# A gated feed-forward tile is split one iteration later, its low part on GpSimd

## The chip, the cores and the metric

The kernel runs on one core of one Trainium2 chip. The metric is the device time in microseconds (us) of one execution, as the median of several. Engines are named as in the profile: PE is TensorE (matmuls), PEld its weight loads, DVE is VectorE, ACT is ScalarE, POOL (Pool) is GpSimd, SP issues most DMAs.

## The reference

A decoder trunk of two layers over 256 positions of width 1024. Each layer has a mixer (the first one gMLP beside RWKV-7, the second dilated attention) and then a gated feed-forward with a causal convolution of width 3. The change is in the feed-forward alone:

```
def conv_glu_ffn(h, w_up, conv_w, conv_b, w_down):
    z = h @ w_up                       # 1024 -> 2 * 2816
    z1 = shift_prev(z)
    z2 = shift_prev(z1)
    z = conv_w[0] * z2 + conv_w[1] * z1 + conv_w[2] * z + conv_b
    gate, val = jnp.split(z, 2, axis=-1)
    return (jax.nn.silu(gate) * val) @ w_down
```

## The kernel before

Every large matrix product is made from three products of rounded parts. A float32 operand is split into a high part (ACT copies it to the rounded type, line 287 or 246) and a low part (the operand minus the high part, a subtraction by `tt`, line 177, or line 247); `mm3` then adds high times high, high times low and low times high on PE (line 174). `split(hi, lo, src)` at line 286 does this for activations, `load` at lines 244 to 247 for weights. `tt` issues a two-input operation on DVE unless it is given another engine.

Weights come in pieces of up to 128x1024 values. SP loads a piece into `raw` (4 buffers), ACT makes `whi`, DVE makes `wlo` (4 buffers each). `piece()` hands the next one to the matmuls and asks for those up to two ahead. A buffer of `whi` or `wlo` can be written again when PE is done with the piece four before.

`ffn(l, ...)` handles layer l in a loop over FT = 22 tiles. Tile i is 128 gate channels and 128 value channels by 256 positions. Its two pieces take 48 matmuls into one PSUM tile `pg` (3 buffers). Then:

- DVE scales the sums by the norm's row factors into `z` (`z<-pg,rb`, line 177), and POOL has cleared two columns of `z` before (line 974).
- The convolution writes `y`: per half one ACT operation (line 983) and two on DVE (lines 984 and 985).
- ACT applies SiLU to the gate half of `y` (line 986); POOL multiplies it by the value half (`y<-y`, line 177).
- `split` puts the product into `H`: ACT makes the high part (`hh`, line 287), DVE the low part (`hl`, line 177).

`z` and `y` have 3 buffers each, `H` holds all 22 tiles. In layer 0 eight output tiles follow, 22 `mm3` steps each over `H` (`DOWN`: for the first two outputs, tiles 0 to 7, 8 to 14 and 15 to 21 in turn); they read pieces of 8 or 7 tiles, so of 1024 or 896 columns. In layer 1 `finish` does the down-projection with positions as rows, in 128x512 matmuls. In four iterations of layer 1, PE also transposes a part of the residual, and ACT copies it to `Rt`.

Each engine takes its instructions in one fixed order. In the feed-forward that order comes from the scheduler that builds the program; an instruction that waits holds all that stand behind it on its engine.

Of the kernel before, what the change touches and what calls it, by code (L numbers as in the profile page):

```python
# [8 lines left out]
F32 = mybir.dt.float32  # L9
F32R = mybir.dt.float32r  # L10
I32 = mybir.dt.int32
AF = mybir.ActivationFunctionType
OP = mybir.AluOpType
# [7 lines left out]
FT = 22  # L21
# [138 lines left out]
def body(nc, tc, A, out):  # L160
# [3 lines left out]
    V, S, G, PE, SP = nc.vector, nc.scalar, nc.gpsimd, nc.tensor, nc.sync  # L164
# [11 lines left out]
    def tt(o, a, b, op, eng=None):  # L176
        (eng or V).tensor_tensor(o, a, b, op)  # L177
# [14 lines left out]
    def P(k, i=0):  # L192
        return pc[:, _PC[k] + i:_PC[k] + i + 1]
# [39 lines left out]
    def piece():  # L233
        i = used[0]
        used[0] += 1
        while len(made) < min(len(plan), i + 1 + AHEAD):
            made.append(make_piece(*plan[len(made)]))
        w, made[i] = made[i], None
        return w
# [43 lines left out]
                    SP.dma_start(cst[:, :NCE], A["cst"][:, :NCE])  # L283
        return (hi[:, :sz].rearrange("p (k n) -> p k n", k=k), lo[:, :sz].rearrange("p (k n) -> p k n", k=k))

    def split(hi, lo, src):
        S.activation(hi, src, AF.Copy)  # L287
        tt(lo, src, hi.bitcast(F32), OP.subtract)

    def mm3(o, w, wk, ncol, x, xk, start, stop):  # L290
        wh, wl = w[0][:, wk, ncol], w[1][:, wk, ncol]
        xh, xl = x[0][:, xk], x[1][:, xk]
        mm(o, wh, xh, start, False)
        mm(o, wh, xl, False, False)
        mm(o, wl, xh, False, stop)
# [31 lines left out]
    def norm_stats(n, p1=None):  # L327
        if p1 is None:
            p1 = ps.tile([128, 512], F32, name="pst", tag="m", bufs=5)
            p1 = [p1[:, b:b + 1] for b in range(2)]  # L330
            norm_sum(p1, n["acc"], True, True)
        rs = sm.tile([128, 2], F32, name="rs", tag="rs", bufs=2)
        for b in range(2):
            V.tensor_scalar(rs[:, b:b + 1], p1[b], 1.0 / D, 1e-6, op0=OP.mult, op1=OP.add)
        G.tensor_tensor(rs, rs, C("nhalf", 16)[:, 0:2], OP.pow)
        n["rs"] = rs

    def norm_rows(n):
        rs = n["rs"]
        p2 = ps.tile([128, 512], F32, name="prb", tag="m", bufs=5)  # L340
        for b in range(2):
            mm(p2[:, 128 * b:128 * b + 128], rs[:, b:b + 1].to_broadcast([128, 128]), ident)
        rb = sm.tile([128, T], F32, name="rb", tag="rb", bufs=2)
        V.tensor_copy(rb, p2[:, 0:T])
        n["rb"] = rb
        n["rb2"] = rb[:, None, :].to_broadcast([128, 2, T])

    def gps():
        return ps.tile([128, 2, T], F32, name="pg", tag="g", bufs=3)

    def mps():
        return ps.tile([128, 512], F32, name="pm", tag="m", bufs=5)

    def gemm_fm(o, x):

        for g in range(2):
            w = piece()
            for k in range(KT):
                mm3(o[:, g], w, k, slice(0, 128), x, k, k == 0, k == KT - 1)
                yield 327  # L360

    def gemm_first(o, x):

        ws = [piece(), piece()]
        for ks in (range(0, 5), range(5, KT)):
            for g in range(2):
                for k in ks:
                    mm3(o[g], ws[g], k, slice(0, 128), x, k, k == 0, k == KT - 1)
                    yield 327
# [21 lines left out]
    def out_tile(n, gname, d, psrc):  # L391
        tt(R[:, d], R[:, d], psrc, OP.add)
        norm_tile(n, X, gname, d)


    def layer_even(nxt):
# [57 lines left out]
        def projections():  # L454
# [85 lines left out]
            for b in range(2):  # L540
                pp = mps()
                for g in range(4):
                    mm(pp[:, 128 * g:128 * g + 128], vt[:, b, 128 * g:128 * g + 128], wst[:, g])
                bs = slice(128 * b, 128 * b + 128)
                mx = t2("mxd").rearrange("p a (b t) -> p (a b) t", b=2)
                for g in range(4):
                    V.scalar_tensor_tensor(mx[:, g], pp[:, 128 * g:128 * g + 128], P("ln_g", g), bs_[:, g], op0=OP.mult, op1=OP.add)
                tt(u[:, :, bs], mx, u[:, :, bs], OP.mult)
                split(X[0][:, 0:4, bs], X[1][:, 0:4, bs], u[:, :, bs])
                yield 872  # L550
# [290 lines left out]
        def epilogue(h, b, oT):  # L841
            jsl = slice(2 * h, 2 * h + 2)
            bs = slice(128 * b, 128 * b + 128)
            o_ = oT[:, :, bs]
            sqo = sm.tile([128, 2, 128], F32, name="sqo", tag="sqo", bufs=2)
            S.activation(sqo, o_, AF.Square)
            yield ("pe", 0, 0)
            pk = mps()
            for i in range(2):
                mm(pk[:, 2 * i:2 * i + 2], sqo[:, i], C("ind", 2))  # L850
            r2 = sm.tile([128, 4], F32, name="r2", tag="r2", bufs=2)
            rsq(r2, pk[:, 0:4], 1.0 / HD, 64e-5)
            r2e = sm.tile([128, 4, 64], F32, name="r2e", tag="r2e", bufs=1)
            S.copy(r2e, r2[:, :, None].to_broadcast([128, 4, 64]))
            yield ("pe", 430, 0)
            pv = mps()
            for i in range(2):
                mm(pv[:, 128 * i:128 * i + 128], r2e[:, 2 * i:2 * i + 2].rearrange("p a b -> p (a b)"), ident)
            tt(o_, o_, pv[:, 0:256].rearrange("p (j n) -> p j n", j=2), OP.mult)
            tt(o_, o_, gate[:, jsl, bs], OP.mult)  # L860
            tt(o_, o_, v_[:, jsl, bs], OP.add)
            split(YB[h][0][:, :, bs], YB[h][1][:, :, bs], o_)
            yield ("pe", 440, 0)
            if b == 1:
                when[f"yb{h}"], WHEN[f"yb{h}"] = clock[0], cnt[0]
# [91 lines left out]
    def ffn(l, n, nxt, gname):  # L957
        pool = tc.tile_pool(name=f"ff{l}", bufs=1)
        fp = pool.__enter__()
        H = [fp.tile([128, FT, T], F32R, name=f"h{x}{l}") for x in "hl"]  # L960
        if l == 1:
            Rt = fp.tile([128, 2, D], F32, name="Rt")
            last["pool"] = fp
        for i in range(FT):
            o = [gps()[:, 0], gps()[:, 0]] if i == 0 else gps()
            for y_, _ in enumerate(gemm_first(o, X) if i == 0 else gemm_fm(o, X)):
                if i == 0 and y_ == 9:
                    norm_stats(n)
                if i == 0 and y_ == 14:
                    norm_rows(n)  # L970
            z = fp.tile([128, 2, T + 2], F32, name="z", tag="z", bufs=3)
            if i == 0:
                fp.tile([128, 248], F32, name="pad_z")
            G.memset(z[:, :, 0:2], 0.0)  # L974
            if i == 0:
                for g in range(2):
                    tt(z[:, g, 2:T + 2], o[g], n["rb"], OP.mult)
            else:
                tt(z[:, :, 2:T + 2], o, n["rb2"], OP.mult)
            y = fp.tile([128, 2, T], F32, name="y", tag="y", bufs=3)  # L980
            for g in range(2):
                ch = i + FT * g
                S.activation(y[:, g], z[:, g, 2:T + 2], AF.Identity, scale=P(f"cw{l}2", ch), bias=P(f"cb{l}", ch))  # L983
                V.scalar_tensor_tensor(y[:, g], z[:, g, 1:T + 1], P(f"cw{l}1", ch), y[:, g], op0=OP.mult, op1=OP.add)  # L984
                V.scalar_tensor_tensor(y[:, g], z[:, g, 0:T], P(f"cw{l}0", ch), y[:, g], op0=OP.mult, op1=OP.add)  # L985
            S.activation(y[:, 0], y[:, 0], AF.Silu)  # L986
            tt(y[:, 0], y[:, 0], y[:, 1], OP.mult, G)
            split(H[0][:, i], H[1][:, i], y[:, 0])
            if l == 1 and i in (2, 3, 4, 5):
                b, e = i % 2, (i - 2) // 2  # L990
                pt = mps()
                for d in range(4):
                    PE.transpose(pt[:, 128 * d:128 * d + 128], R[:, 4 * e + d, 128 * b:128 * b + 128], ident)
                S.copy(Rt[:, b, 512 * e:512 * e + 512], pt)
        if l == 1:
            finish(H, fp, Rt)
            pool.__exit__(None, None, None)
            return
        os = {}
        for d, k0, kn in DOWN:  # L1000
            if k0 == 0:
                os[d] = gps()[:, 0]
            w = piece()
            for k in range(kn):
                mm3(os[d], w, k, slice(0, 128), H, k0 + k, k0 + k == 0, k0 + k == FT - 1)
            if k0 + kn == FT:
                out_tile(nxt, gname, d, os.pop(d))
        pool.__exit__(None, None, None)
# [189 lines left out]
    n3 = norm_new()  # L1198
    layer_odd(n2, n3)
    ffn(1, n3, None, None)  # L1200
    ctx.close()

# [12 lines left out]
```

## Time and profile before

| | us |
|---|---|
| median of 3 runs (674.57 to 676.83) | 675.12 |
| the profiled execution | 676.43 |
| its span, first to last instruction | 674.7 |
| PE busy (5766 matmuls) | 644.9 (96%) |
| DVE busy (946 instructions) | 509.2 (75%) |
| ACT busy (710) | 394.5 (58%) |
| POOL busy (154) | 108.8 (16%) |

The up-projection loop of layer 0 lies at about 183 to 312 us of the span, its down-projection reaches to about 372 us, the loop of layer 1 lies at about 486 to 613 us. Busy shares are means over all stages; the chain that ended last and the waits inside one stage tell more. Ends of matmuls are modelled and overlap, so the distance from start to start is the pace of PE.

### The profile page before, as it was taken

To read this page: it belongs to the slowest core of one execution; us is meant where nothing else is said; L and a number is where in the kernel's file an instruction comes from. 1 tells how busy PE (TensorE), PEld (TensorE's weight loads), DVE (VectorE), ACT (ScalarE), POOL (GpSimd) and SP (SyncE) were. 2 spreads that over 40 slices of the span, in tenths; PEclk is the share of its full clock that TensorE was granted. 3 is DMA by queue.
4 is the path that set the end of the run, shared out by engine and by line. 5 is a ranking of instruction groups with operands and counts; after the bars stand their busy time and mean duration, and the time that the engine had idled before them with its cause. 6 is when DMAs were issued, how large, how long until landed. Compare 5 with 4: busy or idle time off the path is not lost.

```text
span 674.7 us, 14452 instructions
## 1 busy us (share of the span) xinstructions
PE 644.9 (96%) x5766; PEld 615.4 (91%) x5766; DVE 509.2 (75%) x946; ACT 394.5 (58%) x710; POOL 108.8 (16%) x154
## 2 busy tenths in 40 slices
PE   7998989799899999999999999999999999999996
PEld 6888767679899999999999999998999999998896
DVE  6899966747888888888766379886888888888653
ACT  6776432324666666666544468766576666666531
POOL 4100000110422222221112000001222222221000
PEclk9998999879999999999999999999999999999998
DMA  7747264203455555555767553332755555555741
GB/s 250 249 145 235 71 177 103 64 2 126 139 174 177 171 185 175 172 176 167 248 195 222 164 181 126 125 126 95 236 186 177 184 168 177 187 164 195 235 126 63
DMA packets 44916, 110.33 MB, mean 164 GB/s; under 512 B 16433, under 2 KB 18097, under 8 KB 44849
## 3 DMA queue, kind: packets, MB, share of 16 engines
q1 hardware_dynamic: 31104, 105.03, 48.3%
q10 hardware_dynamic: 13584, 3.86, 2.3%
q8 instruction: 45, 0.74, 0.5%
q0 software_dynamic: 160, 0.52, 0.3%
q14 instruction: 23, 0.18, 0.1%
HBM read 106.50 MB, written 2.90 MB: 162 GB/s over the span
## 4 chain that ended last, share of the span: by engine, by line
PE 65%; DVE 20%; POOL 5%; ACT 4%; issue 3%; DMA 3%; SPq 0%; POOLq 0%; ACTq 0%; DVEq 0%
PE pg L174 50%; PE pm L174 14%; DVE wlo L247 6%; POOL y L177 3%; DVE WR L177 2%; DVE y L984 2%; DVE z L177 2%; ACT y L986 1%; DVE y L985 1%; ACT hh L287 1%; DMA scrA<-BK 1%; DVE ftmp L177 1%; PE pm L1135 1%; DVE xl L304 1%; DMA R<-xT 1%
## 5 line engine op out<-in xcount | busy, mean ns | idle before, releaser
L174 PE MATMUL pg<-xh,whi 128*128 128x256 f32 x1008 | 290.0, 288 | 0.6 <-ACT whi L246 0.6
L174 PE MATMUL pg<-xh,wlo 128*128 128x256 f32 x1008 | 284.4, 282 | 2.3 <-DVE wlo L247 2.3
L174 PE MATMUL pg<-xl,whi 128*128 128x256 f32 x1008 | 284.3, 282 | 0.1
L247 DVE TENSOR_TENSOR wlo<-raw,whi 128x1024 fp32r<-128x1024 f32 (+2 forms) x199 | 233.9, 1181 | 46.8 <-ACT whi L246 46.3
L246 ACT ACTIVATE whi<-raw 128x1024 fp32r<-128x1024 f32 (+2 forms) x199 | 200.7, 1017 | 72.2 <-PE pg L174 48.8
L174 PEld LDWEIGHTS pg<-xh,whi 128*128 128x128 f32 x1008 | 192.5, 191 | 6.3 <-issue 3.9
L174 PEld LDWEIGHTS pg<-xh,wlo 128*128 128x128 f32 x1008 | 190.9, 189 | 3.1 <-DVE wlo L247 3.1
L174 PEld LDWEIGHTS pg<-xl,whi 128*128 128x128 f32 x1008 | 192.7, 191 | 0.8 <-DVE xl L300 0.3
L177 POOL TENSOR_TENSOR y<-y 128x256 f32<-128x256 f32 x44 | 63.6, 1445 | 29.2 <-ACT y L986 28.7
L287 ACT ACTIVATE hh<-y 128x256 fp32r<-128x256 f32 x44 | 18.4, 417 | 71.2 <-POOL y L177 71.2
L983 ACT ACTIVATE y<-z,pc 128x256 f32<-128x256 f32 x88 | 48.2, 595 | 9.0 <-DVE z L177 3.9
L177 DVE TENSOR_TENSOR hl<-y,hh 128x256 fp32r<-128x256 f32 x44 | 18.7, 425 | 45.3 <-ACT hh L287 45.3
L174 PE MATMUL pg<-hh,wlo 128*128 128x256 f32 x176 | 49.1, 279 | 0.6 <-DVE wlo L247 0.6
L174 PE MATMUL pg<-hh,whi 128*128 128x256 f32 x176 | 48.7, 277 | 0.0
L174 PE MATMUL pg<-hl,whi 128*128 128x256 f32 x176 | 48.7, 277 | 0.0
L177 POOL TENSOR_TENSOR sqacc<-sqacc,sq 128x256 f32<-128x256 f32 x21 | 18.6, 886 | 162.0 <-ACT sq L312 161.5
L984 DVE SCALAR_TENSOR_TENSOR y<-z,pc,y 128x256 f32<-128x256 f32 x88 | 38.6, 479 | 0.8 <-ACT y L983 0.8
L985 DVE SCALAR_TENSOR_TENSOR y<-z,pc,y 128x256 f32<-128x256 f32 x88 | 38.7, 478 | 0.1
L174 PEld LDWEIGHTS pg<-hh,wlo 128*128 128x128 f32 x176 | 33.0, 188 | 1.3 <-DVE wlo L247 1.2
L174 PEld LDWEIGHTS pg<-hh,whi 128*128 128x128 f32 x176 | 33.1, 188 | 0.0
L174 PEld LDWEIGHTS pg<-hl,whi 128*128 128x128 f32 x176 | 33.1, 188 | 0.0
L974 POOL MEMSET z<- 128x4 f32 x44 | 4.2, 103 | 170.2 <-ACT y L986 151.9
(247 smaller groups left out, 1041.4 us busy)
## 6 DMA issues: line engine op xcount, KB each, us to landing
raw<-w_up SPq DMA_DIRECT2D x88, 512.0 KB, 3.5
raw<-w_dn SPq DMA_DIRECT2D x30, 512.0 KB, 4.1
raw<-w_qkv SPq DMA_DIRECT2D x24, 512.0 KB, 4.0
raw<-w_in SPq DMA_DIRECT2D x20, 512.0 KB, 4.9
raw<-w_dn SPq DMA_DIRECT2D x16, 448.0 KB, 3.9
raw<-ev_wo SPq DMA_DIRECT2D x8, 512.0 KB, 3.8
raw<-od_wo SPq DMA_DIRECT2D x8, 512.0 KB, 3.9
R<-xT SPq DMA_DIRECT2D x4, 256.0 KB, 3.9
```

What stands on the lines that cost most here:

```text
L174: PE.matmul(o, l, r, start=start, stop=stop, skip_group_check=shared)
L177: (eng or V).tensor_tensor(o, a, b, op)
L246: S.activation(hi[:, c], raw[:, c], AF.Copy)
L247: last["lo"] = V.tensor_tensor(lo[:, c], raw[:, c], hi[:, c].bitcast(F32), OP.subtract).ins
L287: S.activation(hi, src, AF.Copy)
L304: V.scalar_tensor_tensor(x[1][:, k], R[:, k], P(gname, k), x[0][:, k].bitcast(F32), op0=OP.mult, op1=OP.subtract)
L974: G.memset(z[:, :, 0:2], 0.0)
L983: S.activation(y[:, g], z[:, g, 2:T + 2], AF.Identity, scale=P(f"cw{l}2", ch), bias=P(f"cb{l}", ch))
L984: V.scalar_tensor_tensor(y[:, g], z[:, g, 1:T + 1], P(f"cw{l}1", ch), y[:, g], op0=OP.mult, op1=OP.add)
L985: V.scalar_tensor_tensor(y[:, g], z[:, g, 0:T], P(f"cw{l}0", ch), y[:, g], op0=OP.mult, op1=OP.add)
L986: S.activation(y[:, 0], y[:, 0], AF.Silu)
L1135: PE.transpose(pt[:, 128 * i:128 * i + 128], sc[:, 128 * i:128 * i + 128], ident)
```

## The change

Inside the loop, tile i's `split` no longer follows its own gating. The tile is kept in a dictionary `ys`, and one iteration later its high part is queued on ACT behind the SiLU of the next tile (`issue_after` fixes that order on ACT), and its low part goes to POOL instead of DVE. The last tile is still split at once, on ACT and DVE.

```diff
-    def split(hi, lo, src):
+    def split(hi, lo, src, eng=None):
         S.activation(hi, src, AF.Copy)
-        tt(lo, src, hi.bitcast(F32), OP.subtract)
+        tt(lo, src, hi.bitcast(F32), OP.subtract, eng)
...
+        ys = {}
         for i in range(FT):
...
-            S.activation(y[:, 0], y[:, 0], AF.Silu)
+            silu = S.activation(y[:, 0], y[:, 0], AF.Silu).ins
             tt(y[:, 0], y[:, 0], y[:, 1], OP.mult, G)
-            split(H[0][:, i], H[1][:, i], y[:, 0])
+
+            ys[i] = y
+            if i > 0:
+                with tc.issue_after(silu):
+                    split(H[0][:, i - 1], H[1][:, i - 1], ys.pop(i - 1)[:, 0], G)
+            if i == FT - 1:
+                split(H[0][:, i], H[1][:, i], ys.pop(i)[:, 0])
```

Seven lines are new ahead of the loop's convolution and SiLU, so line 984 of before is 985 after, 985 is 986, 986 is 987 and 974 is 975. The order of PE's and of SP's instructions is the same in both programs. On DVE, in the middle of the loop of layer 0 (`hl_2260` and `hh_2259` are the two parts of `H`), before:

```order
301 L247 TENSOR_TENSOR wlo<-raw,whi 128x1024
302 L177 TENSOR_TENSOR hl_2260<-y,hh_2259 128x256
303 L177 TENSOR_TENSOR z<-pg,rb 128x2x256
304 L247 TENSOR_TENSOR wlo<-raw,whi 128x1024
305 L984 SCALAR_TENSOR_TENSOR y<-z,pc,y 128x256 x2
306 L985 SCALAR_TENSOR_TENSOR y<-z,pc,y 128x256 x2
```

and now:

```order
303 L247 TENSOR_TENSOR wlo<-raw,whi 128x1024
304 L177 TENSOR_TENSOR z<-pg,rb 128x2x256
305 L247 TENSOR_TENSOR wlo<-raw,whi 128x1024
306 L985 SCALAR_TENSOR_TENSOR y<-z,pc,y 128x256 x2
307 L986 SCALAR_TENSOR_TENSOR y<-z,pc,y 128x256 x2
```

Nothing of the split stands in DVE's queue any more, but for the last tile of each layer. On POOL, at the same place, before:

```order
60 L177 TENSOR_TENSOR y<-y 128x256
61 L974 MEMSET z 128x2x2
62 L177 TENSOR_TENSOR y<-y 128x256
63 L974 MEMSET z 128x2x2
64 L177 TENSOR_TENSOR y<-y 128x256
```

and now:

```order
61 L975 MEMSET z 128x2x2
62 L177 TENSOR_TENSOR y<-y 128x256
63 L177 TENSOR_TENSOR hl_2260<-y,hh_2259 128x256
64 L975 MEMSET z 128x2x2
65 L177 TENSOR_TENSOR y<-y 128x256
66 L177 TENSOR_TENSOR hl_2260<-y,hh_2259 128x256
```

Each `y<-y` of one tile is followed by the low part of the tile before it. On ACT, at the end of the loop of layer 0 (the last two tiles and the first pieces of the down-projection), before:

```order
282 L983 ACTIVATE y<-z,pc 128x256 x2
283 L246 ACTIVATE whi<-raw 128x896
284 L986 ACTIVATE y<-y 128x256
285 L287 ACTIVATE hh_2259<-y 128x256
286 L246 ACTIVATE whi<-raw 128x896
```

and now:

```order
281 L984 ACTIVATE y<-z,pc 128x256 x2
282 L246 ACTIVATE whi<-raw 128x896
283 L987 ACTIVATE y<-y 128x256
284 L287 ACTIVATE hh_2259<-y 128x256 x2
285 L246 ACTIVATE whi<-raw 128x896
```

The `hh` behind a SiLU is now that of the tile before it, and at the end two of them stand in a row, of the last tile but one and of the last.

## Rows read from the trace of the kernel before

**Rows 1.** Chain that ended last, one period of layer 0's loop: start, duration (us), what

```profile
260.61 1.48 POOL y L177
262.11 0.43 ACT hh L287
262.90 0.68 DVE z L177
263.59 1.15 DVE wlo L247
265.96 0.43 ACT y L986
```

**Rows 2.** Windows: length, each engine's busy time (instructions), PE clock, DMA share, GB/s

```profile
190.44:310.57 120.13, 120.08 (x1020) 119.87 (x1019) 98.20 (x161) 77.30 (x122) 32.07 (x39) 1.00 0.54 174
318.00:372.00 54.00, 54.00 (x476) 54.00 (x477) 36.44 (x42) 28.08 (x40) 9.63 (x12) 1.00 0.71 217
```

**Rows 3.** Timeline of DVE, layer 0's loop: start, duration, instruction, idle before and releaser

```profile
190.44 0.69 DVE L177 TENSOR_TENSOR z<-pg,rb 128x512 f32<-128x512 f32 x1 [0.34 <-PE pg L174]
310.57 0.68 DVE L177 TENSOR_TENSOR z<-pg,rb 128x512 f32<-128x512 f32 x1
```

**Rows 4.** Timeline of PE's weight loads, layer 0, behind the loop's last up-projection

```profile
306.17 0.19 PEld L174 LDWEIGHTS pg<-hl,whi 128*128 128x128 f32 x1
306.62 0.19 PEld L174 LDWEIGHTS pg<-hh,wlo 128*128 128x128 f32 x1 [0.26 <-DVE wlo L247]
...
311.62 0.19 PEld L174 LDWEIGHTS pg<-hl,whi 128*128 128x128 f32 x1
312.31 0.19 PEld L174 LDWEIGHTS pg<-hh,wlo 128*128 128x128 f32 x1 [0.50 <-DVE wlo L247]
...
314.59 0.19 PEld L174 LDWEIGHTS pg<-hl,whi 128*128 128x128 f32 x1
314.89 0.19 PEld L174 LDWEIGHTS pg<-hh,wlo 128*128 128x128 f32 x1
...
317.24 0.19 PEld L174 LDWEIGHTS pg<-hl,whi 128*128 128x128 f32 x1
317.90 0.19 PEld L174 LDWEIGHTS pg<-hh,wlo 128*128 128x128 f32 x1 [0.47 <-DVE wlo L247]
```

**Rows 5.** The same timeline behind layer 1's loop, and that loop's window

```profile
620.56 0.19 PEld L174 LDWEIGHTS pm<-wlo,hh 128*128 128x128 f32 x1 [0.18 <-DVE wlo L247]
...
492.39:612.70 120.31, 120.31 (x998) 119.14 (x997) 98.34 (x163) 78.84 (x127) 32.06 (x39) 1.00 0.55 176
```

**Rows 6.** Timelines of POOL and DVE, three places where POOL's two-input operation ran

```profile
190.42 0.75 POOL L177 TENSOR_TENSOR y<-y 128x256 f32<-128x256 f32 x1 [1.23 <-ACT y L986]
...
272.21 1.22 DVE L247 TENSOR_TENSOR wlo<-raw,whi 128x1024 fp32r<-128x1024 f32 x1
272.56 1.47 POOL L177 TENSOR_TENSOR y<-y 128x256 f32<-128x256 f32 x1
...
343.85 1.23 DVE L247 TENSOR_TENSOR wlo<-raw,whi 128x1024 fp32r<-128x1024 f32 x1 [0.61 <-ACT whi L246]
344.66 1.01 POOL L177 TENSOR_TENSOR sqacc<-sqacc,sq 128x256 f32<-128x256 f32 x1 [6.47 <-ACT sq L312]
344.99 0.96 DVE L304 SCALAR_TENSOR_TENSOR xl<-R,pc,xh 128x256 fp32r<-128x256 f32 x1
```

**Rows 7.** Timelines of ACT and DVE around tile 1 of layer 0

```profile
193.20 1.06 ACT L246 ACTIVATE whi<-raw 128x1024 fp32r<-128x1024 f32 x1 [0.47 <-ACT y L983]
194.25 0.42 ACT L986 ACTIVATE y<-y 128x256 f32<-128x256 f32 x1
194.53 1.22 DVE L247 TENSOR_TENSOR wlo<-raw,whi 128x1024 fp32r<-128x1024 f32 x1
```

**Rows 8.** Windows where each layer's up-projection starts, columns as in rows 2

```profile
180.00:186.00 6.00, 5.36 (x32) 5.16 (x32) 4.26 (x7) 2.12 (x2) 1.62 (x1) 0.72 0.61 191
480.00:486.00 6.00, 5.33 (x46) 5.12 (x45) 3.69 (x7) 2.43 (x4) 2.03 (x6) 1.00 0.86 291
```

## The prediction

> **What bounds the kernel now.** I read the chain that ended last first. In layer 0's loop it doesn't run through PE but around a circle of three engines: POOL multiplies `y` (260.61), ACT makes `hh` (262.11), DVE, which had to wait for `hh` before it could take `hl`, scales the next `z` (262.90), makes a `wlo` (263.59), convolves, ACT takes the SiLU (265.96), and POOL follows [rows 1]. Each tile's split so holds DVE back from the next tile.
>
> The second view says what that circle costs. In the 120.13 us from the scaling of tile 1 to that of tile 21, PE is busy for 120.08 us and starts 1020 matmuls [rows 2]. That is 0.1178 us for each; the 20 tiles between need 20 x 48 = 960, and the other 60 already belong to the down-projection. So PE needs 48 x 0.1178 = 5.65 us for a tile and the circle takes 120.13 / 20 = 6.01 us. At the start, DVE waited 0.34 us for PE, so it was not behind; at tile 21 it is behind by 60 x 0.1178 = 7.07 us [rows 3]. PE doesn't stand still for that in the loop, since it runs ahead on weights that were split early. The loop is thus bound by two things at once: PE sets the time, the circle eats up PE's stock of split weights.
>
> The bill comes at the end of the loop, where PE waits for the `wlo` that stand in DVE's late queue [rows 4]. There are four places. From the weight load before to the one that came late it took 0.45, 0.69, 0.30 and 0.66 us, 2.10 in all, where the pace would be 4 x 0.118 = 0.47. **PE lost 1.63 us there.** Behind that, PE is busy for the whole 54.00 us of the down-projection [rows 2]. In layer 1 the loop's window is busy for 120.31 of 120.31 us, and there is a single wait for a `wlo` behind it, of 0.18 us [rows 5].
>
> **The change part by part.**
>
> *Removed from DVE:* 42 of the 44 `hl` (one per tile but for each layer's last), with the wait for `hh` in front of each. The circle is cut: `z` of the next tile stands behind a `wlo` alone. DVE's busy time per tile was 98.20 / 20 = 4.91 us [rows 2]; it was the wait that made 6.01 of it. Without them DVE needs less than PE's 5.65, so it follows PE and never falls behind. PE's order and SP's are unchanged, no matmul goes away and no DMA. The gain is then what PE waited at the ends of the loops and no more: 1.63 + 0.18 = **1.81 us**. The other 20 x 0.36 us that the circle loses are hidden behind a busy PE and are worth nothing.
>
> *Moved to ACT's place behind the next SiLU:* the same 44 `hh`, 0.43 us each [rows 1]. ACT no longer waits for POOL there, so the move costs nothing; ACT's own work is 77.30 / 20 = 3.87 us per tile [rows 2].
>
> *Added to POOL:* 42 two-input operations of 128x256. The trace has no `hl` on POOL. The nearest rows are POOL's `y` and `sqacc`, same size, and they differ: 0.75, 1.47 and 1.01 us [rows 6]. Set beside DVE's rows they tell why. The 0.75 ran beside a DVE operation that reads PSUM (`z`, 190.44 [rows 3]), and neither was longer than usual. The 1.47 began at 272.56, while a `wlo` with both inputs in SBUF ran, whose work ends at 272.21 + 1.15 = 273.36; 0.67 us after that `y` was done. The third began at 344.66 inside a `wlo` that ended at about 345.0, and was done 0.67 later; the DVE operation with two SBUF inputs that was issued at 344.99 then took 0.96 us and ended 0.28 behind POOL. So two-input operations of the two engines pass one after the other, and POOL's own work is 0.67 to 0.75 us. Bounds for one `hl`: 0.67 from below, 1.47 from above if the row's whole length were work. I take 0.7, since it is the value that explains all three.
>
> Does POOL then hold DVE up? Tile 1 was on time, so it shows the steady state that I expect [rows 7]. Counted from the start of its `z` at 190.44: a `whi` starts at 2.76 (its buffer comes free only as PE finishes one more piece, 24 x 0.118 = 2.83), SiLU runs from 3.81 to 4.23, a `wlo` from 4.09 to 5.24. POOL's `y` is issued at about 4.35, passes behind the `wlo` and ends near 5.95. The moved `hh` is long there (4.23 + 0.43 = 4.66), so `hl` runs from 5.95 to 6.65. In that time DVE does the next `z`, at 5.65, from PSUM, beside POOL. The next two-input operation on DVE is a `wlo` whose `whi` has to wait for PE to finish a piece at 5.65 and takes 1.06, so it starts at 6.7. `hl` fits into the hole with about 0.05 us to spare, and if it doesn't, DVE has 5.65 - 5.24 = 0.41 us of its own idle time per tile. Nothing is lost until POOL's delay exceeds that by more than 0.36, the drift that is there now.
>
> *Held longer:* `y` of tile i is read by POOL one tile later, so its buffer (3 of them) comes free at about 6.65 after the next tile's `z`; the writer is tile i + 3 on ACT, two tiles after that. No wait. At the end, the last `hh` stands on ACT behind POOL's last `y`, at about 5.95 after the last `z`, with a `whi` for the down-projection's sixth piece behind it. PE by its order first does five pieces, 8 + 8 + 7 + 7 + 7 steps of three matmuls or 111 x 0.118 = 13.1 us; that `whi` and its `wlo` are done by about 8.5. `H` of the last two tiles is wanted in the sixth and seventh step of the fifth piece, 12.4 us or more behind that `z`, and is there at about 7. Both are covered by 4 us or more; without the cover each would be a stall of that size.
>
> **The sum.** The profiled execution took 676.43 us, 1.3 above the median of 675.12. 676.43 - 1.81 = 674.62 for it, and for the median 675.12 - 1.81 = **673.3 us**, 0.27% less. A difference under 0.3% (2.0 us) is about what a measurement of this kernel can't tell from none. So the change does what it says, the gain is real by the trace, and it lies just inside that bound.
>
> **The rivals.**
>
> *The drift stays in part* (0.16). If `hl` lands on the `wlo` behind `z`, DVE loses up to 0.7 us per tile, 0.41 of it idle anyway, so 0.29 of drift remain where 0.36 were. 20 x 0.29 = 5.8 us instead of 7.07, so the waits shrink by 1.3 at most, and could by less. Against it speaks the hole of [rows 7]; for it, that the hole is only as long as `hl`. Time: 673.9 to 674.9.
>
> *POOL becomes the bound: slower* (0.05). If 1.47 us were POOL's own work and it kept DVE's two-input operations out for all of it, a tile would need 2 x 1.47 = 2.94 us of POOL beside DVE's 4.91 - 0.42 (`hl`) - 0.68 (`z`) = 3.81, so 6.75 us, a drift of 1.1 per tile. Over 20 tiles that is 22 us; from 7.07 the stall now grows one for one, so 15 us more in each layer: about 705 us. It turns slower where the two POOL operations take together over 6.01 - 3.81 = 2.2 us. The 0.75 of [rows 6] speaks against it. The Trainium skill's page "Perfetto Trace Analysis" (Optimizing Scalar/DVE Operations) warns that DVE and GpSimd share an SBUF read port, so that moving work between the two might not help; the rows show the shared passage, but also that the moved operation falls into a time where DVE reads PSUM.
>
> *PE's clock falls once more* (0.11). Ahead of layer 0's first tile, PE stood and was then granted 0.72 of its speed on average in 180 to 186 us; at the same place of layer 1 it stood less and kept 1.00 [rows 8]. Everything there now comes 1.6 us earlier. If layer 1 fell to the level of 1.2 GHz as layer 0 did, 0.28 x 6 = 1.7 us would go and eat the gain: 675.0. The wait in front of it doesn't change, so I don't expect it.
>
> *More comes back than was read* (0.08). Waits that depend on where weights stand in the queues at the start of the attention could shorten too: 671 to 672.5. The full 54.00 us between leaves little for that.
>
> **How the numbers follow.** The forecast (672.7 to 674.0) has 0.60, the rivals 0.16, 0.05, 0.11 and 0.08. The bound of 0.3% is at 673.1, a little under the forecast, and runs differ by more than that distance: I give 0.4 of the forecast's 0.60 and all of the last rival to "faster", 0.32. "Slower" is POOL as the bound and a small part of the clock's case, 0.07. The rest is 0.61. The range of 8 in 10 takes in the drift and the clock above and the first half of the last rival below: 671.8 to 675.6.
>
> **What would show it.** Right: `z` one tile after the other at 5.65 us instead of 6.01, with waits for PE in front of it; no weight load behind layer 0's loop that waits for `wlo`; POOL with `y` and `hl` back to back, `hl` of about 0.7 us. The moved step is wrong if `wlo` behind `z` starts when `hl` ends, or `z` still comes later than PE. The sum is wrong if the four late weight loads stay though DVE is on time (then it was the transfer or ACT that they waited for), or if the down-projection of layer 0, busy throughout before, shows new gaps.

## The result, and the profile after

The changed kernel takes **670.82 us** (median; 20 runs, 664.22 to 677.61). The kernel before took 676.65 us (20 runs, 674.57 to 678.24). The ratio is **0.9896, 95% interval 0.9875 to 0.9918**: 1.0% faster, where 0.3% was forecast, and below the range. Five of the changed kernel's 20 runs (674.83 to 677.61) are so far above its fastest that the ratio leaves them out (with them the medians stand at 0.9914, 0.9% faster); the one profile of this kernel taken at such a time (678.34 us) shows the slower of the two paces that are told of below.

The profiled execution took 672.47 us, 3.96 less than that of before (676.43). The windows of the changed kernel cover the 19 tiles from the scaling of tile 2 of layer 0 to that of tile 21, its down-projection behind that, and a part of layer 1's loop (columns as in [rows 2]):

```profile
197.44:300.81 103.37, 103.37 (x914) 103.37 (x913) 87.95 (x134) 70.60 (x115) 42.97 (x57) 1.00 0.60 192
300.81:360.33 59.52, 59.52 (x527) 59.52 (x526) 38.57 (x44) 30.66 (x43) 8.78 (x9) 1.00 0.65 196
523.00:600.00 77.00, 77.00 (x656) 77.00 (x655) 64.19 (x97) 51.14 (x82) 29.18 (x39) 1.00 0.58 186
```

PE is busy throughout, as in [rows 2], at the same granted clock of 1.00. But a tile of layer 0 takes 103.37 / 19 = **5.44 us**, not the 5.65 that I forecast: a matmul takes 103.37 / 914 = 0.1131 us where before it took 0.1178. In layer 1 it takes 77.00 / 656 = 0.1174, the old pace. So the trace of one and the same kernel holds two paces for the same matmul at the same clock.

The timeline of DVE in the changed kernel shows who waits for whom (start, duration, instruction, idle before and releaser), over one period of layer 0 and one of layer 1:

```profile
251.84 0.69 DVE L177 TENSOR_TENSOR z<-pg,rb 128x512 f32<-128x512 f32 x1 [0.46 <-PE pg L174]
252.88 1.23 DVE L247 TENSOR_TENSOR wlo<-raw,whi 128x1024 fp32r<-128x1024 f32 x1 [0.34 <-ACT whi L246]
254.02 0.88 DVE L985 SCALAR_TENSOR_TENSOR y<-z,pc,y 128x256 f32<-128x256 f32 x2
255.60 1.22 DVE L247 TENSOR_TENSOR wlo<-raw,whi 128x1024 fp32r<-128x1024 f32 x1
257.28 0.69 DVE L177 TENSOR_TENSOR z<-pg,rb 128x512 f32<-128x512 f32 x1 [0.46 <-PE pg L174]
...
596.34 0.69 DVE L177 TENSOR_TENSOR z<-pg,rb 128x512 f32<-128x512 f32 x1 [0.63 <-PE pg L174]
602.00 0.69 DVE L177 TENSOR_TENSOR z<-pg,rb 128x512 f32<-128x512 f32 x1 [0.63 <-PE pg L174]
```

Each `z` now waits for PE, still in the last tiles; in [rows 3] the later `z` had long found its sums done. No `hl` stands on DVE here. The groups of POOL's instructions in layer 0's loop (count, busy us, mean ns, then idle time before) and two rows of POOL's timeline:

```profile
L177 POOL TENSOR_TENSOR y<-y 128x256 f32<-128x256 f32 x22 | 31.2, 1417 | 11.7 <-ACT y L987 10.8
L177 POOL TENSOR_TENSOR hl<-y,hh 128x256 fp32r<-128x256 f32 x20 | 14.9, 744 | 0.0
...
250.52 1.46 POOL L177 TENSOR_TENSOR y<-y 128x256 f32<-128x256 f32 x1
251.94 0.74 POOL L177 TENSOR_TENSOR hl<-y,hh 128x256 fp32r<-128x256 f32 x1
```

`hl` takes 744 ns, as the shortest of [rows 6], stands back to back with `y`, and begins within 0.1 us of DVE's `z` at 251.84, which keeps its 0.69 us.

Where the 3.96 us went: from the first `z` to the last matmul of layer 0's down-projection it is 187.79 to 360.33 = 172.5 us, against 185.89 to 364.95 = 179.1 before, so 6.5 less. In this execution the part ahead of that was 1.9 us longer, with the same code. The attention between took 123.3 us in both. From layer 1's first `z` to the end it took 187.0 us, against 186.4 before: layer 1 gained nothing here, it lost 0.6. (The counts of a window include one or two matmuls that only touch its edges.)

### The profile page after: what moved, and what is told of

Read it like the earlier page. It is cut to its first block, busy times and chain, and to the rows that moved or that the text cites. A ratio compares the mean times of both kernels' runs of the same rounds, so it can differ in the third digit from the quotient of the medians.

```text
span 670.6 us, 14493 instructions
## 1 busy us (share of the span) xinstructions
PE 642.1 (96%) x5766; PEld 613.1 (91%) x5766; DVE 500.4 (75%) x904; ACT 390.6 (58%) x710; POOL 136.4 (20%) x196
## 4 chain that ended last, share of the span: by engine, by line
PE 79%; DVE 12%; DMA 3%; issue 2%; ACT 1%; POOL 1%; ACTq 1%; SPq 0%; POOLq 0%; DVEq 0%
PE pg L174 63%; PE pm L174 14%; DVE wlo L247 3%; DVE WR L177 2%; DMA scrA<-BK 1%; DVE ftmp L177 1%; PE pm L1142 1%; DVE xl L304 1%; DMA R<-xT 1%; DMA at<-scrA 1%; DMA raw<-w_up 1%; ACTq L706 0%; PE prb L174 0%; DVE BK L662 0%; POOL r L321 0%
## 5 line engine op out<-in xcount | busy, mean ns | idle before, releaser
L177 POOL TENSOR_TENSOR y<-y 128x256 f32<-128x256 f32 x44 | 61.7, 1401 | 27.7 <-ACT y L987 26.8
L177 DVE TENSOR_TENSOR z<-pg,rb 128x512 f32<-128x512 f32 (+1 forms) x46 | 30.5, 667 | 21.3 <-PE pg L174 21.3
L177 POOL TENSOR_TENSOR hl<-y,hh 128x256 fp32r<-128x256 f32 x42 | 31.2, 742 | 0.0
```

## The experiments

The theory that the texts on record call FLOOR: PE does the 128x256 matmul, with its weight load, at one of two paces, 113.3 or 117.8 ns, and keeps one for a whole stretch. The circle of three engines ([rows 1], 5.97 us per tile once it turns steadily) lay above both, 48 x 0.1133 = 5.44 and 48 x 0.1178 = 5.65 us, and so was a floor under the loop that hid the pace. The deferral removes the floor, and then the time shows the pace. The rivals: that POOL's relief of DVE makes the gain, and that the faster pace is luck of an execution, which the kernel before could have drawn as well.

**The deferral without POOL** (in the changed kernel):

```
-                    split(H[0][:, i - 1], H[1][:, i - 1], ys.pop(i - 1)[:, 0], G)
+                    split(H[0][:, i - 1], H[1][:, i - 1], ys.pop(i - 1)[:, 0])
```

> Only the deferral: the split of a gated tile comes one iteration later, behind the next SiLU, but its low part stays on DVE. Theory FLOOR: the three-engine circle (6.01 us per tile) was a floor under the loop, and PE has two paces, 113.3 and 117.8 ns per matmul, of which it keeps one for a whole loop; cutting the circle is all that counts. DVE then needs 4.9 us per tile, less than 48 x 113.3 ns = 5.44, so this is as fast as the changed kernel: 664 to 677 us from run to run, median 669 to 673. Rival POOL: the faster pace of PE comes from taking the low part off DVE; then PE stays at 117.8 ns and the time is 673 to 676.

Measured: 670.1 us (8 runs, 667.91 to 677.29), ratio 0.9926 (0.9888 to 0.9964), beside the 0.9914 that the changed kernel has over all its runs. The window over 19 tiles of this kernel and three rows of its DVE:

```profile
195.43:298.45 103.02, 103.02 (x911) 103.02 (x910) 94.77 (x154) 70.50 (x115) 35.14 (x36) 1.00 0.61 192
...
253.25 1.22 DVE L247 TENSOR_TENSOR wlo<-raw,whi 128x1024 fp32r<-128x1024 f32 x1
254.38 0.42 DVE L177 TENSOR_TENSOR hl<-y,hh 128x256 fp32r<-128x256 f32 x1
254.93 0.69 DVE L177 TENSOR_TENSOR z<-pg,rb 128x512 f32<-128x512 f32 x1
```

`hl` is back on DVE, in front of `z`, but waits for nothing, since its `hh` is a tile old. 103.02 / 19 = 5.42 us per tile: the deferral alone does it.

**POOL without the deferral** (in the kernel before):

```
-            split(H[0][:, i], H[1][:, i], y[:, 0])
+            split(H[0][:, i], H[1][:, i], y[:, 0], G)
```

> Only the other engine: the low part on POOL, but the split at once, as before. Theory FLOOR: the circle now closes through ACT, whose high part still waits for POOL's product and has a weight piece behind it: SiLU 0.43, POOL 1.95 with its wait, high part 0.43, whi 1.05, wlo 1.15, convolution 1.2, so about 6.2 us per tile. That is a floor like that of before: 674 to 680 us with a small spread. Rival POOL: PE at 113.3 ns, 664 to 673.

Measured: 677.19 us (12 runs, 675.53 to 678.99), ratio 1.0009 (0.9995 to 1.0023). DVE is relieved (494.4 us busy in its profile, where it was 509.2) and nothing is gained. The timelines of this kernel's ACT and DVE, one turn:

```profile
268.70 0.42 ACT L287 ACTIVATE hh<-y 128x256 fp32r<-128x256 f32 x1 [1.71 <-POOL y L177]
269.02 1.04 ACT L246 ACTIVATE whi<-raw 128x1024 fp32r<-128x1024 f32 x1
...
270.10 1.22 DVE L247 TENSOR_TENSOR wlo<-raw,whi 128x1024 fp32r<-128x1024 f32 x1 [1.43 <-ACT whi L246]
...
272.54 0.42 ACT L986 ACTIVATE y<-y 128x256 f32<-128x256 f32 x1 [0.54 <-DVE y L985]
274.68 0.42 ACT L287 ACTIVATE hh<-y 128x256 fp32r<-128x256 f32 x1 [1.72 <-POOL y L177]
```

The circle goes on through ACT: `hh` waits for POOL, the `whi` behind it and then DVE's `wlo` come late, then the convolution, SiLU and POOL. From `hh` to `hh` it is 274.68 - 268.70 = 5.98 us (6.2 was expected). The wait that has to go is ACT's for POOL, and of the two halves of the change only the deferral removes it.

**Both kernels once more**, unchanged, to see whether an execution draws its pace.

> The kernel before, unchanged, once more, for a second profile. Theory FLOOR: 674.5 to 678.5 us whatever PE's pace; if this profile has a loop at 113.3 ns, its tiles still come every 5.97 us and the waits for weights behind that loop add up to more, up to 6 us instead of 1.6. Rival POOL: PE is at 117.8 ns in both loops.

> The changed kernel, unchanged, for a second profile. Theory FLOOR: each loop is either at 113.3 or at 117.8 ns by chance and its tiles come every 5.44 or 5.65 us; the time is about 664 with both fast, 670 to 672 with one, 676 with none. Rival POOL: layer 0 at 113.3 and layer 1 at 117.8 as in the first profile, 670 to 672.

Measured: 678.11 and 678.34 us (one run each). The kernel before: two windows of its layer 0 loop, then a weight load and two `z` between them from the timelines:

```profile
198.79:253.00 54.21, 54.21 (x481) 54.21 (x480) 44.49 (x74) 34.95 (x55) 14.21 (x18) 1.00 0.56 177
260.00:312.00 52.00, 50.34 (x418) 48.54 (x418) 42.29 (x71) 32.88 (x53) 13.98 (x16) 1.00 0.53 169
...
254.47 0.19 PEld L174 LDWEIGHTS pg<-xh,wlo 128*128 128x128 f32 x1 [0.42 <-DVE wlo L247]
...
252.59 0.68 DVE L177 TENSOR_TENSOR z<-pg,rb 128x512 f32<-128x512 f32 x1
258.56 0.68 DVE L177 TENSOR_TENSOR z<-pg,rb 128x512 f32<-128x512 f32 x1
```

This time PE began at 54.21 / 481 = 0.1127 us and ran ahead; at 254.47 its stock of split weights was used up, and from there it stood still once per tile. `z` comes every 5.97 us all the same. The floor, seen directly: the fast pace was there, and bought nothing. The changed kernel, in the same two stretches as above:

```profile
196.78:304.19 107.41, 107.41 (x914) 107.41 (x913) 89.02 (x133) 70.54 (x115) 41.90 (x57) 1.00 0.59 184
304.00:366.00 62.00, 62.00 (x529) 62.00 (x528) 38.68 (x44) 30.69 (x43) 8.80 (x9) 1.00 0.64 188
```

107.41 / 914 = 0.1175 us in the loop, 62.00 / 529 = 0.1172 behind it: no wait for a `wlo` anywhere, and yet no faster than before. With `z` on time, and PE at 5.65 us per tile, it is the kernel of my forecast, and shows the second half of my mistake, below.

**The floor put back** (in the changed kernel): three more operations on DVE per tile, behind the convolution, whose result nobody reads, so that DVE has more work than PE.

```
+        scr = fp.tile([128, T], F32, name="scr")
...
+            with tc.issue_after(conv):
+                for _ in range(3):
+                    V.scalar_tensor_tensor(scr, z[:, 1, 0:T], P(f"cw{l}0", ch), y[:, 1], op0=OP.mult, op1=OP.add)
```

> The changed kernel with three idle convolution steps more per tile on DVE (0.40 us each, written to a scratch tile that nothing reads), which neither ACT nor POOL waits for. DVE then needs 4.5 + 1.2 = 5.7 us per tile, up to 6.5 where it passes behind POOL's operations. Theory FLOOR: the floor is back without the circle; tiles come every 5.75 to 6.5 us whatever PE's pace, PE waits for weights at the end of the loop or once per tile, and the time is 675 to 695 us, tile time and waits fitting each other. If only PE's pace by itself mattered, the time would stay at 664 to 678 with a median near 671.

Measured: 694.48 us (4 runs, 692.55 to 695.61), ratio 1.0262 (1.0237 to 1.0287). A window of this kernel's loop and two `z`:

```profile
240.00:300.00 60.00, 58.90 (x474) 55.27 (x473) 60.00 (x100) 36.05 (x60) 25.26 (x30) 1.00 0.53 172
...
255.78 0.68 DVE L177 TENSOR_TENSOR z<-pg,rb 128x512 f32<-128x512 f32 x1
261.90 0.68 DVE L177 TENSOR_TENSOR z<-pg,rb 128x512 f32<-128x512 f32 x1
```

DVE is busy for 60.00 of 60.00 us and the tiles come every 6.12 us (6.62 in layer 1), though nearly all of PE's stretches in this loop ran at 113.3 ns. A floor above PE sets the time, also where it is built of work, not of waits.

**The pace asked for.** In the six profiles up to here, the matmuls behind the attention's 64-column matmuls ran at 113.3 ns. (That those behind every broadcast ran at 117.8, as the expectation below has it, is not so: layer 0's first loop stands behind one, with a stretch at half clock at its start, and ran at 113.3 in three of the six.) So I put two small, unneeded matmuls of 64 columns ahead of each loop's stretch and behind the four transposes in layer 1, in the changed kernel and in the one before:

```
+    def drain():
+        pd = mps()
+        for q in (slice(0, 64), slice(64, 128)):
+            mm(pd[q, 0:64], ident[:, 0:64], ident[:, 0:64])
```

> The changed kernel with two idle matmuls of 64x64 (nothing reads their result) behind the norm's broadcast at the start of each loop and behind the four transposes in layer 1. In six profiles PE ran at 113.3 ns per matmul behind every stretch of 64-column matmuls in the attention and at 117.8 behind every broadcast or transpose. Theory FLOOR with the pace set by what PE did last: both loops and layer 0's down-projection run at 113.3, tiles every 5.44 us in both layers, 663 to 667 us with a small spread. If the pace is chance: as the changed kernel, 664 to 678, plus about 0.5.

> The kernel before with the same idle matmuls. Theory FLOOR: PE may start at 113.3 ns but uses up its stock of split weights in some 13 tiles and then waits once per tile; tiles stay at 5.97 us and the time stays at 674 to 679, as without them. If the circle were no floor, both loops would gain from the pace and the time would be 664 to 670.

Measured: the changed kernel so drained takes 668.53 us (6 runs, 666.04 to 675.84), ratio 0.989 (0.9848 to 0.9932). That misses the 663 to 667 of "what PE did last", and two of the six runs lie above 675: both fit the expectation's other case, a pace drawn by chance. The kernel before so drained takes 677.37 us (12 runs, 673.91 to 678.6), ratio 1.001 (0.9993 to 1.0027). It ran at 113.3 ns from 186.3 us to 258 in layer 0 and from 518 to 591 in layer 1, then waited, and stayed at 5.97 and 5.98 us per tile: a faster PE is worth nothing under the floor. The waits in layer 0 of the drained kernel before (us in all, times, longest):

```profile
PEld pg L174 <- DVE wlo L247: 4.3, 11, 0.5
```

The profiled execution of the drained changed kernel took 675.71 us. Its windows, layer 0's loop and down-projection and then layer 1's loop:

```profile
196.00:304.00 108.00, 108.00 (x919) 108.00 (x918) 89.82 (x135) 71.30 (x117) 42.09 (x57) 1.00 0.58 185
305.20:367.20 62.00, 62.00 (x529) 62.00 (x528) 38.65 (x44) 30.69 (x43) 8.83 (x9) 1.00 0.63 188
522.00:606.00 84.00, 84.00 (x743) 84.00 (x742) 71.19 (x109) 57.52 (x93) 33.45 (x45) 1.00 0.60 193
```

Layer 1 runs at 84.00 / 743 = 0.1131, layer 0 at 0.1175. Its drain had stood in front of a stretch at half clock (181.4 to 188.2 us), and behind that the pace came out slow. (In the drained kernel before, the same drain with a shorter such stretch behind it, 182.4 to 185.8 us, was followed by the fast pace.) So I put one more drain behind layer 0's first tile, and one ahead of the attention's values:

```
+            if l == 0 and i == 1:
+                drain()
```

> The changed kernel with the idle 64x64 matmuls of the run before, and two places more: behind tile 1 of layer 0, where PE is back at full clock, and behind the norm's broadcast at the start of the attention layer. Theory FLOOR with the pace set by what PE did last: the loops of both layers at 113.3 ns and 5.44 us per tile in every execution, 664 to 668 us, none above 670. If the pace is chance, some executions stay above 672, as four of six of the run before were not.

Measured: 668.8 us (6 runs, 667.02 to 671.63), ratio 0.9882 (0.9853 to 0.9912). No run is left near 675, but one is above the 670 expected, and the median is 0.8 us above the expected 664 to 668. In the profile both loops run fast, layer 0's at 100.00 / 884 = 0.1131 us:

```profile
200.00:300.00 100.00, 100.00 (x884) 100.00 (x884) 84.96 (x130) 67.93 (x112) 42.11 (x55) 1.00 0.60 193
515.00:598.00 83.00, 83.00 (x734) 83.00 (x734) 70.22 (x107) 57.16 (x93) 33.07 (x45) 1.00 0.60 192
```

The same with the low part on DVE (the edit of the first experiment on top), to ask about POOL again where the pace disturbs less:

> The same, but the low part of the deferred split on DVE instead of POOL. With PE's pace held fast this weighs the second half of the change by itself. Theory FLOOR: DVE needs 4.9 us of the 5.44 per tile, so the same as the run beside it within 0.3 per cent, 664 to 668 us. Rival POOL: DVE falls behind by up to 0.5 us per tile and the time is 668 to 676.

Measured: 667.13 us (6 runs, 665.86 to 674.83), ratio 0.9874 (0.9835 to 0.9914). One of these six runs took 674.83 us, so slow executions still occur. The intervals of the two overlap: whether the low part is on POOL or on DVE can't be told from the time.

And with three drains in all: the two just added, and of the others only the one behind the last of layer 1's four transposes:

```
-                    drain()
...
-                drain()
+                if i == 5:
+                    drain()
```

> The changed kernel with idle 64x64 matmuls at three places alone: behind tile 1 of layer 0, behind the broadcast of the attention layer, and behind the last transposes of layer 1 (tile 5). In layer 1 the tiles with transposes came 6.37 us apart with the idle matmuls and 6.09 without, where the pace alone would have taken off 0.22, so one place costs about 0.5 us. Five places less save 2.5; the first six tiles of layer 1 go back to 117.8 ns and cost 6 x 0.22 = 1.3. Theory FLOOR with the pace set by what PE did last: 667 to 668.5 us median, none above 672; layer 0 at 5.44 us per tile from tile 2 on, layer 1 at 5.65 to tile 5 and 5.44 from tile 6 on. If the pace is chance: executions above 674 come back.

Measured: 671.25 us (6 runs, 665.19 to 672.91), ratio 0.9907 (0.9874 to 0.994). Missed. In the profile layer 1 went on at 117.8 ns behind its only drain (at 510.14), window of this kernel:

```profile
530.00:596.00 66.00, 66.00 (x562) 66.00 (x562) 54.80 (x83) 43.13 (x70) 26.15 (x35) 1.00 0.59 185
```

Over the five profiles of kernels with drains, 23 of 28 drains at full clock were followed by 113.3 ns and 5 by 117.8, among these all three ahead of the attention's values. Without a drain there, the start of layer 1's loop came out at 117.8 in seven profiles (two of before, two of the changed kernel, the first two experiments and the last one), but the kernel with the floor put back, which has no drain either, shows 113.3 at 4 of 5 such places. So a drain in layer 1's loop shifts the odds and doesn't settle them, and it costs about 0.5 us each. What decides the pace stays open.

## Why the prediction was wrong, point by point

**Right: what the change does to the order and the waits.** The circle is cut, `z` follows PE, and no weight load behind layer 0's loop waits for `wlo`. `hl` takes 0.744 us (forecast 0.7), back to back with `y` and beside a `z` that reads PSUM. POOL is not the bound, and the shared passage of [rows 6] costs nothing that the trace shows. The Trainium skill's page "Perfetto Trace Analysis" (Optimizing Scalar/DVE Operations) warns that moving work between DVE and GpSimd might not help. The runs agree: the two drained kernels, with `hl` on POOL and on DVE, can't be told apart (668.8 and 667.13 us), and the move without the deferral gained nothing (ratio 1.0009). The covers at the end of the loop held: PE is busy for 59.52 of 59.52 us behind it. The clock did not fall at layer 1's start: from 480 to 486 us it was granted at 1.00 (in [rows 8] as well), PE busy throughout. "The drift stays in part", "POOL becomes the bound" and "PE's clock falls once more" did not happen. (The clock did fall there in the profile of the kernel with POOL but no deferral: 0.72 from 484 to 490 us, and the layer between took 125.2 us instead of 123.3. So the 1.7 us of that rival were of the right size.)

**Wrong: the step "PE needs 48 x 0.1178 = 5.65 us for a tile", and what stood on it, "the other 20 x 0.36 us that the circle loses are hidden behind a busy PE and are worth nothing".** 0.1178 us is what PE took in that execution, not what it needs. The runs showed two paces. With the floor gone, a loop at the fast one gains 1056 x 4.5 ns = 4.75 us, and layer 0's down-projection, 528 matmuls, is worth 2.3 us (59.73 or 62.07 us). So the 0.36 us per tile that the circle lost were worth something: they kept the fast pace from showing.

My own rows had it. In [rows 2] the loop has 120.13 / 1020 = 0.1178, and the down-projection, the same kind of matmul at the same clock of 1.00, 54.00 / 476 = 0.1134. (That window takes in some 7 us too much: the down-projection ends at 364.95 us, not at about 372, and up to there the pace is 46.95 / 415 = 0.1131.) I took both for one pace, and used 0.118 for the down-projection as well. Those 4.5 ns, over one loop, are more than twice the 1.81 us that I forecast.

**Also wrong: the bill of 1.63 us in [rows 4] as a pure gain.** The waits were also breaks, and behind them the down-projection of before ran at 113.3 ns, in each trace of before. Where the changed kernel's loop runs slowly, the down-projection has no break and stays slow: it takes 62.07 us without a wait, where that of before took 61.60 with all its waits. That is the run of 678.34 us. In layer 1, where 0.18 us was to come back, it is the same: behind the loop the 132 matmuls of 128x512 take 30.57 us in both profiles of the changed kernel, and took 30.27 in both of the kernel before. So with a slow PE, as I assumed it, that trace shows no gain at all; the gain is in the executions in which PE is fast.

The executions side by side (a tile is the distance of two `z` in the steady loop, the stretch in the fourth column ends with the start of the last matmul):

| execution profiled | us | layer 0, tile | first `z` to end of down-projection | down-projection | layer 1, tile |
|---|---|---|---|---|---|
| before | 676.43 | 5.97 | 179.1 | 61.60 | 5.98 |
| before, again | 678.11 | 5.97 | 178.7 | 61.69 | 5.98 |
| before, drained | 677.35 | 5.97 | 181.4 | 61.69 | 5.98 |
| POOL, not deferred | 678.99 | 5.97 | 178.8 | 61.61 | 5.98 |
| changed | 672.47 | 5.44 | 172.5 | 59.73 | 5.65 |
| changed, again | 678.34 | 5.65 | 179.5 | 62.07 | 5.65 |
| deferred on DVE | 669.75 | 5.44 | 172.7 | 59.73 | 5.65 |
| changed, drained | 675.71 | 5.65 | 182.9 | 62.07 | 5.44 |
| changed, drained late | 668.05 | 5.44 | 175.6 | 59.73 | 5.44 |
| the same, low part on DVE | 665.86 | 5.44 | 174.7 | 59.73 | 5.44 |
| changed, three drains | 671.06 | 5.44 | 172.4 | 59.73 | 5.65 |
| floor put back | 692.55 | 6.12 | 183.2 | 63.47 | 6.62 |

Everything with the circle in it is at 5.97 or 5.98, at either pace; without it, and without added work, a tile takes 5.44 or 5.65. (The drained kernels' stretches also hold the drains.)

**The rival "more comes back" (0.08)** had the right side and the wrong reason: it named waits at the start of the attention, and nothing was found there. **The range** was too narrow for the same cause as the forecast: it varied the waits and held PE's pace fixed.

**Left open:** what sets the pace. The runs show that without the circle a fast pace counts, not that the change makes it more frequent; the profiles are too few to say how often each pace is drawn. No execution near 664 us was profiled, so that both loops are fast there is not shown. The kernels with drains have lower medians than both kernels here (668.8 and 667.1 against 670.82 and 676.65 us), but their intervals overlap that of the changed kernel.

## What to carry to other kernels

An engine that is busy all the time is not proof that the work around it is hidden: divide its busy time by its instructions in every stretch, and if the same instruction at the same clock has two durations, the slower one is not what the engine needs. A circle through several engines is a floor under a loop; compare its period with the fastest pace of the busy engine anywhere in the trace, and look for the wait that closes it (here ACT's for POOL, behind which DVE waits for ACT) instead of the engine with the most work. And a wait that is removed may also have been a break that something later profited from, so the stretch behind it belongs in the sum.

## What the runs showed of the hardware

At a granted clock of 1.00 PE does the 128x256 matmul with a weight load every 113.3 or every 117.8 ns, and holds one of them through as many as some 1500 matmuls. Most changes of pace came at breaks: a wait, a stretch at half clock, transposes or matmuls of another width. In three traces it also changed without a break, where the two operands of the matmuls change sides (in the run with the late drains from 117.8 to 113.3 ns at 383.5 us, PE busy throughout). Identical code drew different paces in different executions (5.44 and 5.65 us per tile in the two profiles of the changed kernel), and one execution can have one pace in layer 0 and the other in layer 1. That spread, 664 to 678 us, was hidden as long as the floor lay above it: the kernel before ran within 674.57 to 678.24 in its 20 runs.
